# A decoder layer on one core: token-tile chains into the FFN in a written order on three engines, a third early unit, scale rows on the sync queue, and an opening ordered by hand

## The chip, the cores and the metric

The kernel runs on one core of a Trainium2 chip. The core has five engines that run side by side and wait for each other by semaphores: TensorE (PE, matrix products into PSUM), VectorE (DVE), ScalarE (ACT), GpSimd (POOL) and SyncE (SP). DMAs are issued from SP's and from ACT's queue; an engine that issues a DMA does so in its own order, between its other instructions. The metric is the device time of one execution in microseconds (us); less is better.

## What is computed

One layer of a decoder trunk on 512 tokens of width 1024: a mixer (mLSTM heads beside a gated convolution), then a gated FFN with a causal convolution of three taps. Both are sandwich-normed (an RMS norm before and one after), and scale, shift and gate of each come from a conditioning vector c through the matrix ada_w (adaLN). The parts around the change:

```python
mod = silu(c) @ ada_w[l] + ada_b[l]
sh1, sc1, g1, sh2, sc2, g2 = jnp.split(mod[:, None, :], N_MOD, axis=-1)
u = rms_norm(x, mix_pre_g[l]) * (1.0 + sc1) + sh1
proj = u @ w_in[l]
...
mix = jnp.concatenate([h, y], axis=-1) @ w_out[l]
x = x + g1 * rms_norm(mix, mix_post_g[l])

u = rms_norm(x, ffn_pre_g[l]) * (1.0 + sc2) + sh2
up = causal_dwconv(u @ ffn_up[l], ffn_conv_w[l], ffn_conv_b[l])
a, gt = jnp.split(up, 2, axis=-1)
f = (jax.nn.silu(gt) * a) @ ffn_down[l]
x = x + g2 * rms_norm(f, ffn_post_g[l])
```

D_FF is 2816, so the FFN has 22 units of 128 channels in each of its halves a and gt. All arrays are float32.

## The kernel before

**Precision and tiles.** Every large product is made from operands split into a high and a low part (float32r): `mm3` (L164) issues hi·hi, hi·lo and lo·hi into one PSUM bank. A weight block of 1 MB is loaded by SP into one of two `raw` buffers and split by `w_split` (L142) in four pieces: ACT copies the high part, POOL subtracts it for the low part. Split pieces lie in `wpool` (20 tiles) or in `slots` (44 tiles of 128 x 512, which also hold most activations). PSUM has eight banks: four `mm`, two `at`, and two that belong first to `cps` and later to the `cv` pool.

**Order.** SP and TensorE issue in the order in which the program is written. The order on DVE, ACT and POOL is made by a planner from its own simulated timeline, in which instructions that are written earlier have priority unless a written dependency or a raised priority number says otherwise.

**Opening (L105 to L290).** SP loads c, broadcast to 128 partitions (L105), some vectors (L107), the eight half tiles of x (L209), and then by turns a 1 MB pair of adaLN rows (`first_load`, L199, into the two `raw` buffers) and a block of glu weights (L269). ACT squares the half tiles with a sum (L226); DVE and POOL make a factor for each token (L228, L229); DVE scales the tile (L231); TensorE transposes it (`turn_x`, L218) into eight banks xT0 to xT7, of which xT6 and xT7 need banks that xT0 to xT3 leave. ACT and DVE copy them out by turns (L240, L242). For each of eight blocks k, DVE multiplies the adaLN rows by silu(c) and sums (`junk`, L279), makes scale and shift `gsk` (L282, L283), ACT makes the high part of u and the exact u (L285, L286), POOL its low part (L287), and TensorE runs 18 matmuls into six banks. The later adaLN products (`ada_block`, L125) are loaded by ACT's queue; the planner may put such an issue between ACT's other work.

**Into the FFN (L705 to L788).** The mixer's output is made in two column halves, mixa and mixb, with a bank for each of four token tiles. For mixb the first eight of sixteen weight blocks run over all tiles, then the rest tile by tile (8 x 3 matmuls each). Behind each tile comes its chain, `mix_tile` (L739): sums of squares on ACT (`sq_sum`, L552), a product with the g1 row on DVE, a factor (`token_factor`, L556: DVE, then POOL's power), the new x in two halves (L747), their squares on ACT, a second factor, then u in two steps for each half, a product with factor and the scale row `gs2r` (L752) and the addition of the shift row `sh2r` (L753, the second half on POOL). `turn_tile` (L756) transposes u into two `at` banks, and ACT and DVE make its high and low part. TensorE's order is: last part of mixb for tiles 0, 1, 2, transposes of tile 0, last part of tile 3, transposes of tile 1, then the early units.

The scale rows come by DMA: `send_rows` (L526) transposes the gains and writes them to DRAM, `row` (L535) reads them back broadcast over the partitions, both on ACT's queue. The two early units (0 and 1) run on half the tokens first, all four banks interleaved, with tile 2's transposes in the midst, then on the other half after tile 3's. From unit 2 on, a unit is 48 matmuls of 512 columns. Each unit's two banks are read by `conv3` (L796) on ACT and DVE, and a bank is free for a later unit when that is done. The adaLN products for g2 (blocks 40 to 47) are written at units 4, 8, 12 and 16 and have to follow `last_lo[0]`, an instruction of the last attention head.

## Time and profile before

| | |
|---|---|
| median of 3 runs | 831.38 us (827.21 to 833.15) |
| profiled execution, own time | 833.13 us |
| profiled execution, span from first to last instruction | 831.4 us |
| mean granted TensorE clock | 0.983 |
| HBM read, written | 102.60 MB, 4.21 MB |

The span is what the profile's clock counts; the execution's own time has some 1.7 us around it. A row of a timeline is: start in us, duration in us, engine, line of the kernel, operation, output<-inputs by tile name, shapes, count, and in brackets how long the engine was idle before it and which engine ended the wait. "ACTq" and "SPq" are the issuing of DMAs. A row of the table of windows is: the stretch, its length, then for PE, PE's weight loads, DVE, ACT and POOL the busy time with the number of instructions, then the granted TensorE clock (1.00 is full speed), the share of the DMA engines' time and GB/s.

### The profile page before, as it was taken

What the parts mean: (1) busy time and instruction counts of PE and PEld (TensorE: products, weight loads), DVE (VectorE), ACT (ScalarE), POOL (GpSimd) and SP (SyncE); (2) the same over time, 40 slices, a digit from 0 to 9 for tenths busy, and PEclk for the clock granted to TensorE, in tenths of its full rate; (3) what the DMA queues carried; (4) which work ended last, traced back from release to release, by engine and by line L of the source; (5) the groups of instructions that cost most, each with busy time, mean ns of one, the idle gap of its engine ahead of it and who ended that gap; (6) DMA issues with size and microseconds to landing.
All of it is one profiled execution on the core that took longest, in us unless ns stands there. A gap on an engine that the chain in (4) does not pass through costs nothing.

```text
span 831.4 us, 10237 instructions
## 1 busy us (share of the span) xinstructions
PE 788.3 (95%) x3713; PEld 654.9 (79%) x3713; DVE 473.7 (57%) x735; ACT 380.2 (46%) x710; POOL 448.2 (54%) x362
## 2 busy tenths in 40 slices
PE   3899999999999999999977979999999999999996
PEld 2688897778888888888866858888888888888885
DVE  4748999999997435548447664444444444000004
ACT  5665438757464454740434244444444444222211
POOL 2789749778596442541758334444444444444420
PEclk9999999999999999999988989999999999999999
DMA  7973214121237131518754522222222232222305
GB/s 275 330 274 126 101 52 152 51 90 64 76 103 256 61 113 52 203 51 300 289 196 142 162 102 84 83 91 98 101 102 102 102 126 102 99 83 80 119 1 177
DMA packets 25026, 107.47 MB, mean 129 GB/s; under 512 B 2928, under 2 KB 2960, under 8 KB 17552
## 3 DMA queue, kind: packets, MB, share of 16 engines
q1 hardware_dynamic: 16848, 83.73, 28.2%
q10 hardware_dynamic: 8128, 23.09, 7.8%
q8 instruction: 29, 0.48, 0.2%
q14 instruction: 21, 0.17, 0.1%
HBM read 102.60 MB, written 4.21 MB: 128 GB/s over the span
## 4 chain that ended last, share of the span: by engine, by line
PE 65%; DVE 16%; DMA 8%; issue 6%; POOL 3%; ACT 2%; SPq 0%; DVEq 0%; POOLq 0%; ACTq 0%
PE up L166 9%; PE up L167 9%; PE up L168 9%; DVE cv L605 8%; DMA ada<-in_adaT 5%; PE dn L168 5%; PE dn L166 5%; PE dn L167 5%; PE qko L166 4%; PE qko L168 4%; PE qko L167 4%; PE s L403 2%; PE o L414 2%; PE mixa L168 1%; PE mixa L166 1%
## 5 line engine op out<-in xcount | busy, mean ns | idle before, releaser
L605 DVE SCALAR_TENSOR_TENSOR cv<-gt,cvw,cv 128x488 f32<-128x488 f32 (+20 forms) x200 | 134.2, 725 | 2.8 <-issue 2.3
L872 DVE TENSOR_TENSOR fo<-dn,g2r 128x512 f32<-128x512 f32 x8 | 5.5, 691 | 100.1 <-PE dn L168 100.1
L149 POOL TENSOR_TENSOR wup_1024l<-wup,wup_1024h 128x512 fp32r<-128x512 f32 x22 | 29.4, 1334 | 42.0 <-ACT wup_1024h L148 42.0
L149 POOL TENSOR_TENSOR wup_1536l<-wup,wup_1536h 128x512 fp32r<-128x512 f32 x22 | 30.1, 1367 | 35.0 <-ACT wup_1536h L148 35.0
L601 POOL TENSOR_TENSOR cs<-cs,cs 128x510 f32<-128x510 f32 (+3 forms) x32 | 42.8, 1337 | 6.4 <-PE qko L168 4.5
L166 PE MATMUL up<-u2h,wup_0h 128*128 128x512 f32 (+1 forms) x96 | 37.0, 386 | 6.8 <-DVE fa0c L801 6.3
L149 POOL TENSOR_TENSOR wup_512l<-wup,wup_512h 128x512 fp32r<-128x512 f32 x22 | 28.4, 1289 | 24.5 <-ACT wup_512h L148 24.4
L149 POOL TENSOR_TENSOR wup_0l<-wup,wup_0h 128x512 fp32r<-128x512 f32 x22 | 29.0, 1318 | 19.2 <-ACT wup_0h L148 19.2
L167 PE MATMUL up<-u2l,wup_0h 128*128 128x512 f32 (+1 forms) x96 | 36.8, 383 | 0.7 <-DVE u2l L766 0.7
L168 PE MATMUL up<-u2h,wup_0l 128*128 128x512 f32 (+1 forms) x96 | 36.6, 381 | 0.0
L166 PE MATMUL up<-u2h,wup_512h 128*128 128x512 f32 (+1 forms) x96 | 36.4, 379 | 0.0
L133 DVE SCALAR_TENSOR_TENSOR junk<-ada,cb 128x1024 bf16<-128x1024 f32 x20 | 30.2, 1509 | 10.2 <-DMA ada<-in_adaT 9.9
L167 PE MATMUL up<-u2l,wup_512h 128*128 128x512 f32 (+1 forms) x96 | 36.0, 375 | 0.0
L167 PE MATMUL up<-u2l,wup_1536h 128*128 128x512 f32 (+1 forms) x96 | 35.9, 374 | 0.0
L168 PE MATMUL up<-u2h,wup_512l 128*128 128x512 f32 (+1 forms) x96 | 35.9, 374 | 0.0
L166 PE MATMUL up<-u2h,wup_1536h 128*128 128x512 f32 (+1 forms) x96 | 35.9, 374 | 0.0
L168 PE MATMUL up<-u2h,wup_1536l 128*128 128x512 f32 (+1 forms) x96 | 35.9, 374 | 0.0
L167 PE MATMUL up<-u2l,wup_1024h 128*128 128x512 f32 (+1 forms) x96 | 35.6, 371 | 0.0
L168 PE MATMUL up<-u2h,wup_1024l 128*128 128x512 f32 (+1 forms) x96 | 35.6, 371 | 0.0
L166 PE MATMUL up<-u2h,wup_1024h 128*128 128x512 f32 (+1 forms) x96 | 35.6, 371 | 0.0
L599 ACT ACTIVATE cs<-gt,cvw 128x511 f32<-128x511 f32 (+4 forms) x40 | 27.0, 715 | 9.4 <-POOL cs L601 8.2
L148 ACT ACTIVATE wup_512h<-wup 128x512 fp32r<-128x512 f32 x22 | 13.9, 632 | 37.5 <-PE up L167 35.6
(699 smaller groups left out, 2619.8 us busy)
## 6 DMA issues: line engine op xcount, KB each, us to landing
wup<-in_w_up SPq DMA_DIRECT2D x22, 1024.0 KB, 4.8
wqko<-in_w_qko SPq DMA_DIRECT2D x12, 1024.0 KB, 4.8
wd<-in_w_down SPq DMA_DIRECT2D x11, 1024.0 KB, 4.8
ada<-in_adaT ACTq DMA_DIRECT2D x20, 512.0 KB, 4.6
ada<-in_adaT SPq DMA_DIRECT2D x16, 512.0 KB, 6.5
wo<-in_w_out SPq DMA_DIRECT2D x8, 1024.0 KB, 4.8
spare<-in_adaT ACTq DMA_DIRECT2D x12, 512.0 KB, 7.4
wglu<-in_w_glu SPq DMA_DIRECT2D x5, 1024.0 KB, 6.1
```

The source lines that it names most:

```text
L133: t = V.scalar_tensor_tensor(out=junk, in0=r, scalar=1.0, in1=cb, op0=ALU.mult, op1=ALU.mult, accum_out=mod[:, i : i + 1])
L148: S.activation(hi[:, :n], src, AF.Copy)
L149: G.tensor_tensor(out=lo[:, :n], in0=src, in1=hi[:, :n].bitcast(F32), op=ALU.subtract)
L166: PE.matmul(ps, a[0], b[0], start=start, stop=False)
L167: PE.matmul(ps, a[0], b[1], start=False, stop=False)
L168: PE.matmul(ps, a[1], b[0], start=False, stop=stop)
L403: PE.matmul(sp[:, :n], ks[d][:, cc * P : (cc + 1) * P], qs[d][:, cc * P :], start=d == 0, stop=d == 1)
L414: PE.matmul(o[:, : DH + 2], E[h][cc][:, a : a + P], vs[h][cc], start=cc == 0, stop=cc == tt)
L599: S.activation(t[:, d:], cvx[j][:, : T - d], AF.Copy, scale=w(CK - 1 - d))
L601: G.tensor_tensor(out=side[:, d:], in0=side[:, d:], in1=t[:, d:], op=ALU.add)
L605: last_tap = V.scalar_tensor_tensor(out=cp[:, d:], in0=cvx[j][:, : T - d], scalar=w(CK - 1 - d), in1=cp[:, d:], op0=ALU.mult, op1=ALU.add)
L872: V.tensor_tensor(out=m, in0=banks[tt][hf], in1=g2r[hf], op=ALU.mult)
```

## The change

- **Opening.** c is loaded as two rows of one partition and broadcast by a product with ones on TensorE; both Silu read PSUM. x goes ahead of the vectors, half of it by ACT's queue. The second half of each tile is squared on DVE. All copies out of PSUM are on ACT, in a written order; for k=0 the high part of u is made straight from PSUM and its low part on DVE; for k=0 and 1 the products run in three passes over the six banks.
- **`in_order`.** A block that makes DVE, ACT and POOL issue its instructions in the order in which they are written. Instructions from outside the block may still be placed between them. It is put around the opening and around the chains into the FFN.
- **Chains.** `mix_tile` is cut into `chain_sums`, `chain_x` and `chain_u`; the product with `gs2r` moves ahead of the second factor, and factor and shift are one instruction on DVE. The four chains, the transposes, the splits of units 1 and 2 (low part on DVE) and the early units are written in one order. Three units run on half the tokens, a unit at a time; the third takes the two `cv` banks.
- **Rows.** gs2 and sh2 are written and read by SP's queue, between the loads of units 1 and 2. The g1 rows lie in the pool of v, u in the adaLN pool, and unit 1's weights in `slots`.
- **g2 blocks.** `last_lo[0]` is now the last low part of u2, so the products of blocks 40 to 47 have to follow it.

```diff
+    def in_order():
...
+        for ins in traced[a:]:
+            if ins.engine in (V.engine, S.engine, G.engine):
+                if ins.engine in last:
+                    tc.add_manual_dep(ins, last[ins.engine].name, mybir.DependencyInfo(mybir.DependencyClass.NoSync, mybir.DependencyReason.DATA),
+                                      reason="program order")
+                last[ins.engine] = ins
...
-    nc.sync.dma_start(cb, c.partition_broadcast(P))
...
+    for hf in range(2):
+        nc.sync.dma_start(crow[hf][:1, :], c[hf * T : (hf + 1) * T].rearrange("(a n) -> a n", a=1))
...
+    for tt in range(NT):
+        for hf in range(2):
+            (nc.scalar if hf else nc.sync).dma_start(xn[tt][hf], x[tt * P : (tt + 1) * P, hf * T : (hf + 1) * T])
...
-    S.activation(cps, cb, AF.Silu)
-    S.activation(cb, cb, AF.Silu)
+    for hf in range(2):
+        PE.matmul(cps[:, hf * T : (hf + 1) * T], ones[:1, :], crow[hf][:1, :], start=True, stop=True)
...
+    S.activation(first_silu, zero, AF.Silu)
...
-        G.tensor_tensor(out=lo[:, :n], in0=src, in1=hi[:, :n].bitcast(F32), op=ALU.subtract)
+        (eng or G).tensor_tensor(out=lo[:, :n], in0=src, in1=hi[:, :n].bitcast(F32), op=ALU.subtract)
...
+    first_load(0)
+    nc.sync.dma_start(vec[:, :FIRST], vecs[:, :FIRST])
...
+    def x_scale(tt, xs):
+        for hf in range(2):
+            V.tensor_scalar(out=xn[tt][hf], in0=xn[tt][hf], scalar1=xs[:, 1:], scalar2=None, op0=ALU.mult)
+            for i in range(NT if hf == 0 else 2):
+                turn_x(NT * hf + i, tt)
...
+    opening = in_order()
+    opening.__enter__()
...
     for tt in range(NT):
+        xsq = small.tile([P, 2], F32, tag="adap", name=f"xsq{tt}")
         for hf in range(2):
...
+            xjunk = xjunks[hf]
+            if hf:
+                V.scalar_tensor_tensor(out=xjunk, in0=xn[tt][hf], scalar=1.0, in1=xn[tt][hf], op0=ALU.mult, op1=ALU.mult, accum_out=xsq[:, hf:])
+            else:
+                S.activation(xjunk, xn[tt][hf], AF.Square, accum_out=xsq[:, :1])
+        if tt:
+            x_scale(tt - 1, xss[tt - 1])
+        if tt == 1:
+            S.activation(cb, cps, AF.Silu)
+        if tt == NT - 1:
+            S.activation(cps, cps, AF.Silu)
...
+        V.tensor_scalar(out=xs[:, :1], in0=xsq[:, :1], scalar1=xsq[:, 1:], scalar2=D * EPS, op0=ALU.add, op1=ALU.add)
+        G.tensor_tensor(out=xs[:, 1:], in0=xs[:, :1], in1=mhalf[:, :1], op=ALU.pow)
+        xss.append(xs)
+    x_scale(NT - 1, xss[-1])
...
-    for j in range(KT):
-        if j >= 6:
-            for tt in range(NT):
-                turn_x(j, tt)
-        if j % 2:
+    for j in range(6, KT):
+        for tt in range(NT):
+            turn_x(j, tt)
...
+        if k == 0:
+            for j in range(3):
+                x_out(j, S)
...
+        if k == 0:
+            x_out(3, S)
+            V.tensor_scalar(out=xr[0], in0=xr[0], scalar1=gsk[:, :1], scalar2=gsk[:, 1:], op0=ALU.mult, op1=ALU.add)
         hi, lo = u[k]
-        S.activation(hi, xr[k], AF.Identity, scale=gsk[:, :1], bias=gsk[:, 1:])
-        S.activation(xr[k], xr[k], AF.Identity, scale=gsk[:, :1], bias=gsk[:, 1:])
-        G.tensor_tensor(out=lo, in0=xr[k], in1=hi.bitcast(F32), op=ALU.subtract)
-        u[k] = (hi, lo)
-        for i, ps in enumerate(banks0):
-            mm3(ps, blk(wk, i), u[k], k == 0, k == KT - 1)
+        S.activation(hi, xT_ps[0] if k == 0 else xr[k], AF.Identity, scale=gsk[:, :1], bias=gsk[:, 1:])
+        if k:
+            S.activation(xr[k], xr[k], AF.Identity, scale=gsk[:, :1], bias=gsk[:, 1:])
+        (G if k else V).tensor_tensor(out=lo, in0=xr[k], in1=hi.bitcast(F32), op=ALU.subtract)
+        if k == 0:
+            for j in (6, 7, 4, 5):
+                x_out(j, S)
+        if k < 2:
+            for a, b in ((0, 0), (1, 0), (0, 1)):
+                for i, ps in enumerate(banks0):
+                    PE.matmul(ps, blk(wk, i)[a], u[k][b], start=k == 0 and a == b, stop=False)
+        else:
+            for i, ps in enumerate(banks0):
+                mm3(ps, blk(wk, i), u[k], False, k == KT - 1)
...
+    wide1 = vpool.tile([P, 2 * T + 8], F32, tag="vh", name="g1r")
+    g1r = row(0, lambda n: [wide1[:, :T], wide1[:, T : 2 * T]], "g1")
...
-    send_rows(KT, 2 * KT)
-    gs2r = row(1, cvtile, "gs2")
-    sh2r = row(2, cvtile, "sh2")
...
-    def mix_tile(tt):
+    def chain_sums(tt):
...
         ps = banks[tt]
         sq_sum(ps, msq[:, 2 * tt + 1 : 2 * tt + 2], f"mixb{tt}")
-        mb = slot(f"mgb{tt}")
-        V.tensor_tensor(out=mb, in0=ps, in1=g1r[1], op=ALU.mult)
-        r = token_factor(msq[:, 2 * tt : 2 * tt + 2], f"rm{tt}")
+        un = adas.tile([P, D], F32, tag="ada", name=f"un{tt}")
+        uns[tt] = [un[:, :T], un[:, T:]]
+        V.tensor_tensor(out=uns[tt][1], in0=ps, in1=g1r[1], op=ALU.mult)
+        return token_factor(msq[:, 2 * tt : 2 * tt + 2], f"rm{tt}")
...
+    def chain_x(tt, r):
...
-        for hf, m in enumerate((mg[tt], mb)):
+        for hf, m in enumerate((mg[tt], uns[tt][1])):
             V.scalar_tensor_tensor(out=x1[tt][hf], in0=m, scalar=r, in1=x1[tt][hf], op0=ALU.mult, op1=ALU.add)
             sq_sum(x1[tt][hf], xsq[:, hf : hf + 1], f"x1_{tt}_{hf}")
-        r2 = token_factor(xsq, f"rf{tt}")
-        for hf in range(2):
-            un = slot(f"un{tt}_{hf}")
-            V.scalar_tensor_tensor(out=un, in0=x1[tt][hf], scalar=r2, in1=gs2r[hf], op0=ALU.mult, op1=ALU.mult)
-            (G if hf else V).tensor_tensor(out=un, in0=un, in1=sh2r[hf], op=ALU.add)
-            uns[tt, hf] = un
+        for hf, un in enumerate(uns[tt]):
+            V.tensor_tensor(out=un, in0=x1[tt][hf], in1=gs2r[hf], op=ALU.mult)
+        return token_factor(xsq, f"rf{tt}")
...
+    def chain_u(tt, r):
+        for hf, un in enumerate(uns[tt]):
+            V.scalar_tensor_tensor(out=un, in0=un, scalar=r, in1=sh2r[hf], op0=ALU.mult, op1=ALU.add)
...
     def turn_tile(tt):
-        for hf in range(2):
-            un = uns[tt, hf]
...
+        turned[tt] = [atbank(f"xT{tt}_{hf}") for hf in range(2)]
...
             S.activation(hi, part, AF.Copy)
-            V.tensor_tensor(out=lo, in0=part, in1=hi.bitcast(F32), op=ALU.subtract)
...
-    up_w = {0: w_load(w_up[0], "wup0", slots, "t"), 1: w_load(w_up[1], "wup1")}
-    for tt in range(NT):
+            last_lo[0] = V.tensor_tensor(out=lo, in0=part, in1=hi.bitcast(F32), op=ALU.subtract)
+    def mix_last(tt, a, b):
         for n_, k in enumerate(MIX[KA:]):
-            mm3(banks[tt], (hy[k][0][:, tok(tt)], hy[k][1][:, tok(tt)]), wo[n_], False, n_ == 2 * KT - KA - 1)
-        mix_tile(tt)
-        if tt > 1:
-            turn_tile(tt - 2)
+            if a <= n_ < b:
+                mm3(banks[tt], (hy[k][0][:, tok(tt)], hy[k][1][:, tok(tt)]), wo[n_], False, n_ == 2 * KT - KA - 1)
...
+    def up_split(i, r, pool, tag):
+        q = len(up_w[i])
+        up_w[i].append(w_split(r[:, q * T : (q + 1) * T], f"wup{i}_{q * T}", pool, tag, V))
...
+    NE = 3
...
+    def up_half(th, i, only=None):
+        for half, ps in enumerate(early[i]):
+            if only not in (None, half):
+                continue
+            for k in range(KT):
+                mm3(ps[:, th * HT : (th + 1) * HT], blk(up_w[i], half * KT + k), (u2h[:, th, k, :], u2l[:, th, k, :]), k == 0, k == KT - 1)
...
+    up_w = {0: w_load(w_up[0], "wup0", slots, "t")}
+    raw1 = raw_up(1)
+    send_rows(KT, 2 * KT, nc.sync)
+    gs2r = row(1, cvtile, "gs2", nc.sync)
+    sh2r = row(2, cvtile, "sh2", nc.sync)
+    raw2 = raw_up(2)
+    early += [[mmbank(f"up{i}_{half}") for half in range(2)] for i in range(2)]
+    with in_order():
+        for tt in range(3):
+            mix_last(tt, 0, 2 * KT - KA)
+        up_split(1, raw1, slots, "t")
+        r = chain_sums(0)
+        up_split(1, raw1, slots, "t")
+        r = chain_x(0, r)
+        chain_u(0, r)
+        turn_tile(0)
+        mix_last(3, 0, 7)
+        r = chain_sums(1)
+        up_split(1, raw1, slots, "t")
+        r = chain_x(1, r)
+        chain_u(1, r)
+        turn_out(0)
+        turn_tile(1)
+        mix_last(3, 7, 2 * KT - KA)
+        r = chain_sums(2)
+        turn_out(1)
+        r = chain_x(2, r)
+        up_split(1, raw1, slots, "t")
+        chain_u(2, r)
+        up_half(0, 0)
+        turn_tile(2)
+        r = chain_sums(3)
+        up_split(2, raw2, wpool, "w")
+        r = chain_x(3, r)
+        up_split(2, raw2, wpool, "w")
+        chain_u(3, r)
+        up_half(0, 1)
+        up_split(2, raw2, wpool, "w")
+        early.append([cvbank(f"up2_{half}") for half in range(2)])
+        up_half(0, 2, 0)
+        turn_tile(3)
+        turn_out(2)
+        up_split(2, raw2, wpool, "w")
+        turn_out(3)
+    up_half(0, 2, 1)
+    for i in range(NE):
+        up_half(1, i)
...
-            turn_tile(3)
-        for k in range(KT):
-            if not th and k == KT // 2:
-                turn_tile(2)
-            for ps, i, half in early:
-                mm3(ps[:, th * HT : (th + 1) * HT], blk(up_w[i], half * KT + k), (u2h[:, th, k, :], u2l[:, th, k, :]), k == 0, k == KT - 1)
...
-        if i < 2:
-            pa, pg = early[2 * i][0], early[2 * i + 1][0]
+        if i < NE:
+            pa, pg = early[i]
```

`send_rows` and `row` take the queue as an argument, and use ACT's unless told otherwise.

More of the change, by code (lines that the diff above doesn't have):

```diff
@@ L1 @@
-from contextlib import ExitStack
+from contextlib import ExitStack, contextmanager
 import numpy as np
@@ L67, in decoder_layer @@
     psum = ctx.enter_context(tc.tile_pool(name="psum", bufs=1, space=PSUM))
+    @contextmanager
+    def in_order():
+        traced = nc.cur_bb.bb.instructions
+        first = traced[-1]
+        yield
+        a = next(i for i in reversed(range(len(traced))) if traced[i] is first) + 1
+        last = {}
+        for ins in traced[a:]:
[4 more added lines that the diff above has]
+                last[ins.engine] = ins
     def slot(name, dt=F32):
@@ L216, in decoder_layer, with x_out @@
     V.tensor_scalar(out=g32, in0=vcols("mix_pre_g", 0, KT), scalar1=RD, scalar2=None, op0=ALU.mult)
[L218 to L239 removed]
+    xr = [slot(f"xr{j}") for j in range(KT)]
+    for j in range(6, KT):
+        for tt in range(NT):
+            turn_x(j, tt)
+    def x_out(j, eng):
+        if eng is S:
             S.activation(xr[j], xT_ps[j], AF.Copy)
```

57 lines of the change are left out of this document (25 added, 32 removed).

## The prediction

> **What bounds the kernel now.** I read the page first, then the table of windows (busy time by stretch), then the timeline of each engine where that table shows TensorE idle.
>
> ```profile
> span 831.4 us, 10237 instructions
> PE 788.3 (95%) x3713; PEld 654.9 (79%) x3713; DVE 473.7 (57%) x735; ACT 380.2 (46%) x710; POOL 448.2 (54%) x362
> ```
> ```profile
> 0.00:25.00 25.00, 8.77 (x33) 6.35 (x33) 14.28 (x38) 15.06 (x30) 7.90 (x16) 1.00 0.82 288
> 25.00:140.00 115.00, 114.59 (x552) 96.79 (x553) 96.54 (x165) 64.88 (x114) 90.05 (x79) 1.00 0.46 165
> ...
> 428.00:433.00 5.00, 0.36 (x2) 0.19 (x2) 4.50 (x8) 1.38 (x4) 2.83 (x3) 0.86 0.15 57
> ...
> 449.00:456.00 7.00, 2.54 (x16) 2.37 (x15) 5.86 (x8) 0.71 (x3) 4.20 (x5) 0.72 0.41 146
> ...
> 460.00:464.00 4.00, 3.27 (x28) 3.10 (x27) 4.00 (x6) 0.00 (x0) 2.21 (x1) 1.00 0.62 183
> ...
> 468.00:477.60 9.60, 9.56 (x80) 9.36 (x78) 4.64 (x6) 2.34 (x4) 3.20 (x2) 1.00 0.51 170
> 477.60:484.00 6.40, 0.12 (x1) 0.15 (x1) 5.82 (x8) 2.75 (x5) 3.24 (x3) 0.90 0.50 164
> 484.00:490.00 6.00, 6.00 (x15) 4.71 (x16) 3.62 (x6) 1.68 (x3) 0.29 (x1) 0.53 0.01 3
> 490.00:800.00 310.00, 310.00 (x1368) 256.42 (x1368) 103.95 (x124) 120.19 (x196) 146.41 (x114) 1.00 0.26 95
> ```
>
> TensorE is the bound: 310 us without a gap from 490 to 800, 1368 matmuls, 0.227 us each at 512 columns (0.12 us each at 256, 80 in 9.56 us). Only time in which TensorE is idle or at half clock can be won, and the change touches just two such places: the first 25 us, and 428 to 490, where the token tiles pass from the mixer to the FFN. There 428:433, 449:456 and 477.6:484 are nearly empty, and after the pauses the clock column falls (0.53 in 484:490: 15 matmuls in 6 us where 26 would fit, 2.6 us lost).
>
> **The opening, step by step.** Rows of the windows and of the queues' timelines:
>
> ```profile
> 10.00:15.00 5.00, 3.67 (x15) 2.87 (x16) 3.25 (x10) 3.60 (x10) 1.92 (x4) 1.00 1.03 413
> ```
> ```profile
> 6.91 0.63 ACT L226 ACTIVATE xjunk<-xn 128x512 bf16<-128x512 f32 x1 [1.05 <-DMA xn<-in_x]
> ...
> 13.75 0.21 DVE L228 TENSOR_SCALAR xs<-xsq 128x1 f32<-128x1 f32 x1 [0.97 <-ACT xjunk L226]
> 13.88 0.87 DVE L231 TENSOR_SCALAR xn<-xn,xs 128x512 f32<-128x512 f32 x2
> ...
> 14.67 1.21 DVE L279 SCALAR_TENSOR_TENSOR junk<-ada,cps 128x1024 bf16<-128x1024 f32 x1
> ...
> 15.81 1.93 DVE L231 TENSOR_SCALAR xn<-xn,xs 128x512 f32<-128x512 f32 x2
> ...
> 18.92 0.80 SPq L203 DMA_DIRECT2D ada<-in_adaT  x2
> ...
> 25.23 0.80 PE L167 MATMUL glu<-ul,wglu_0h 128*128 128x512 f32 x1 [2.29 <-POOL ul L287]
> ...
> 28.40 0.20 DVE L283 TENSOR_SCALAR gsk<-adap,vec 128x1 f32<-128x1 f32 x1
> ...
> 47.02 3.13 ACTq L131 DMA_DIRECT2D ada<-in_adaT  x1
> ...
> 49.22 0.21 DVE L283 TENSOR_SCALAR gsk<-adap,vec 128x1 f32<-128x1 f32 x1
> ...
> 52.97 1.29 POOL L287 TENSOR_TENSOR ul<-xr,uh 128x512 fp32r<-128x512 f32 x1
> ...
> 59.25 0.39 PE L168 MATMUL glu<-uh,wglu_512l 128*128 128x512 f32 x1
> ```
>
> Before, the first half tile of x lands at 6.91 behind a 512 KB broadcast of c, eight squares run one after the other on ACT until 13.75, and DVE puts an adaLN product (14.67) between the last factor and its two scalings (15.81). Steady matmuls begin at 25.23, with the low part of u from POOL. The change loads c as two rows of 2 KB, which frees 1.3 us of transfer (512 KB at 413 GB/s), gives four of the eight squares to DVE, and keeps the products behind all scalings. The broadcast of c on TensorE and the second Silu from PSUM lie in idle time; vec, moved behind x and the first adaLN load on SP, is first read by bp1, after the last scaling. Four issues of x move to ACT's queue, which has nothing else to do then.
>
> The first tile, both halves, I put at 6.2, the others 1.3 apart (512 KB each). A tile costs DVE 0.7 for its square (half of 1.21, and a readout), 0.9 for two scalings (13.88), 0.2 for the factor: from tile 1 at 7.5 on DVE is the slower one, and tile 3's factor is out at 13.2. 0.96 later (the same three engines as 424.27 to 425.23 below) the scalings, to 14.9; two small operations and two products, 17.6; factors, 18.1; hi of u0 straight from PSUM, 0.8; first glu matmul at 19.2, its lo meanwhile on DVE. For k<2 all hi·hi products go first, so the 2.29 us wait for POOL disappears. With eight matmuls at 0.43 (cold) and ten at 0.227, k=0 ends at 24.9; before, k=1 began 7 x 18 x 0.227 = 28.6 ahead of the last matmul's end, 59.5, at 30.9. So 6 us at this point.
>
> But the later k are fed by two raw buffers of adaLN rows: the load for k=2 leaves when the products of k=0 end (18.92). From k=2 (28.40) to k=7 (49.22) the factors come every 4.16 us, and TensorE eats a k in 18 x 0.227 = 4.09. So what lasts is what the supply gains: 18.9 − 17.6 = 1.3 us, and the slack it had. k=7's lo of u ended at 54.26, late because ACT stood 3.13 us at a DMA issue of a later block (47.02). Without that it is 49.22 + 3.3 (hi, xr and POOL's lo: 0.8, 0.8, 1.29 and gaps) = 52.5, minus 1.3 = 51.2; the last matmul of k=7 starts sixteen later at 54.8, against 59.25: **4.4 us** gained. If ACT stops so again it is 2.7, and 0 if the written order itself stops once on a late load (low ends); if the supply never binds, 6.9 (high end: 6 and the wait's rest). I take 4.4, since the stop is of the planner's making and the loads keep their order. What follows up to 411 goes at TensorE's own pace or on chains that start from it, and shifts with it.
>
> **Into the FFN, step by step.**
>
> ```profile
> 420.17 1.29 POOL L149 TENSOR_TENSOR wup_1536l<-wup,wup_1536h 128x512 fp32r<-128x512 f32 x1
> ...
> 421.44 0.63 ACT L148 ACTIVATE wup_0h<-wup 128x512 fp32r<-128x512 f32 x1 [5.01 <-DMA wup<-in_w_up]
> ...
> 422.96 0.58 ACT L554 ACTIVATE mixb0junk<-mixb 128x512 bf16<-128x512 f32 x1
> ...
> 424.27 0.20 DVE L559 TENSOR_SCALAR rm0t<-msq 128x1 f32<-128x1 f32 x1
> ...
> 425.23 0.75 DVE L747 SCALAR_TENSOR_TENSOR x<-mg,rm0r,x 128x512 f32<-128x512 f32 x1 [0.77 <-POOL rm0r L561]
> ...
> 427.97 0.21 DVE L559 TENSOR_SCALAR rf0t<-xsq 128x1 f32<-128x1 f32 x1 [1.32 <-ACT x_1junk L554]
> ...
> 428.85 1.41 DVE L752 SCALAR_TENSOR_TENSOR un<-x,rf0r,gs2r 128x512 f32<-128x512 f32 x2
> ...
> 432.81 1.97 PE L761 MATMUL xT<-ident,un 128*128 128x128 f32 x8 [4.64 <-DVE un L753]
> ...
> 457.82 1.22 DVE L133 SCALAR_TENSOR_TENSOR junk<-ada,cb 128x1024 bf16<-128x1024 f32 x1
> ...
> 478.12 1.22 DVE L133 SCALAR_TENSOR_TENSOR junk<-ada,cb 128x1024 bf16<-128x1024 f32 x1 [1.58 <-DMA ada<-in_adaT]
> ...
> 481.68 0.74 DVE L801 SCALAR_TENSOR_TENSOR fa0c<-up,vec,fa0c 128x511 f32<-128x511 f32 x1
> ...
> 483.88 0.77 PE L166 MATMUL up<-u2h,wup_0h 128*128 128x512 f32 x1 [6.32 <-DVE fa0c L801]
> ...
> 497.54 0.39 PE L166 MATMUL up<-u2h,wup_0h 128*128 128x512 f32 x1
> ...
> 568.82 0.69 DVE L836 TENSOR_TENSOR fl<-fa8c,fh 128x512 fp32r<-128x512 f32 x1 [0.70 <-ACT fh L835]
> ```
>
> I keep the old clock times. ACT and DVE still begin with the split of unit 1, so with its load at 421.44: SP issues that load as before, and the scale rows wait behind it (issue about 419, 3 to 6 us to land, wanted at 425.7 and 427.8: covered by 1 to 2 us). Behind them SP has only unit 2's load, wanted at 444; ACT loses four issues. A split's lo costs 0.7 on DVE (568.82, the same operation) instead of 1.29 on POOL (420.17), so POOL has only the powers left.
>
> Tile 0: ACT split 0.54 and sums 0.67; DVE split 0.7 and product 0.65, factor at 423.35 (was 424.27); 0.96 to x as before; two x at 0.67, two products at 0.6, factor at 426.9; 0.88 more, and since gs2 now comes ahead of the factor only one step a half is left: transposes at 428.5. The second half waits for the bank of tile 1, freed by its product at 429.8. Done 430.35 (they began at 432.81 before). TensorE: 21 matmuls, 4.76, to 435.1. Tile 1 by the same prices: u at 435.6, banks free when both lo of tile 0 are out at 436.9; TensorE waits 1.2, then transposes and three matmuls to 438.2. From here it no longer waits: 48 x 0.12 = 5.8 a unit and half, transposes 1.1 each: 438.2 + 6 x 5.8 + 2 x 1.1 = **475.2** for unit 3. Tile 2 is ready at 443.8 (wanted 444.0), tile 3 at 450.3 (wanted 453.9). Before, unit 3 began at 497.54, so 22.3 us; the third unit's narrower matmuls (0.6 us more) are in it.
>
> The bank wait (483.88) came from the g2 blocks: eight products with DMA waits on DVE from 457.82, and behind them unit 0's taps at 481.68. Now they follow the last lo of u2 (about 456), and unit 0's taps, ready at 464, are wanted only at 475: 8 us of cover.
>
> The buffers that move (unit 1's halves to the slots, un to the adaLN pool, g1 to the v pool, unit 2's banks from the cv pool) cost no work. The slots just fit: 16 halves of the mixer's last eight blocks, 4 mg, 8 x1 and 16 of units 0 and 1 are 44; a wait would fall on unit 1's fourth split, made at 442 and wanted at 449.
>
> Two deductions. The clock:
>
> ```profile
> 150.00:160.00 10.00, 10.00 (x39) 7.41 (x39) 10.00 (x18) 5.89 (x10) 5.51 (x5) 0.83 0.29 106
> ```
>
> After some tiny matmuls the clock fell here, 39 matmuls instead of 46, 7 x 0.227 = 1.6 us; in 460:464, with 0.7 us idle, it didn't. My two pauses of some 1.2 us lie between: none to two falls, I take one, 1.6. ACT's stores of x1 between the squares: 1.0. 22.3 − 1.6 − 1.0 = **19.7**; bounds 8 (rivals below) and 22.3.
>
> [...]
>
> **Sum:** 4.4 + 19.7 = 24.1. The profiled execution took 833.13 us (span 831.4), 1.75 above the median of the runs; 833.13 − 24.1 = 809.0, against the median 831.38 it is 807.3. I predict 807.3.
>
> **Rivals.** (1) The g2 blocks again ahead of unit 0's taps: DVE is free at 456, and the planner may fill it. Eight blocks took 457.82 to 479.4, so taps about 480.3, bank 2.2 later at 482.5: 7.3 us of wait and 2.6 of clock, 9.9 less, 817. For it: it happened before; against: the taps are ready after two or three blocks. (2) The order doesn't matter, only data: transposes start no earlier than 432.81, and just the bank wait goes: 6.3 + 2.6 − 0.6 = 8.3, with the opening's 4.4 12.7, 819. For it: the same load at 421.44 heads both; against: two of the steps that go, a scaling on DVE and POOL's shift, lie between 427.97 and 432.81. (3) Both of these, or one with no gain in the opening: within 1%, 823 to 831. (4) Slower: the clock stays at half through the short-matmul stretch 428 to 475. That is 24 x 0.227 + 288 x 0.12 = 40 us of work, 40 us more: 847. It decides from 24 us on, 60% of that work. For it: 449:456 and 484:490 at 0.72 and 0.53; against: 460:464, pauses and 256-column matmuls at 1.00.
>
> [...]
>
> **Chances.** Forecast 0.68 (its own range 801 to 813: the high ends together, 29, and 19 gained), rival 1 0.12, rival 2 0.08, rival 3 0.06, rival 4 0.06. The range 799 to 819 holds the first three. A measurement here tells about 1% from no change; faster 0.88, same 0.06, slower 0.06.
>
> **What would show it.** Right: first glu matmul near 19, k=7 ending near 55; tile 0's transposes 47 us before unit 3 (65 before); no bank wait ahead of unit 3; windows of the transition near full at clock 1.00. Wrong: a new wait of ACT or DVE at the head of the written order, ada products ahead of the taps, or a clock near 0.5 over the early units.

## The result, and the profile after

| | before | after |
|---|---|---|
| median of the runs | 830.81 us (827.21 to 833.15, 4 runs) | 805.84 us (805.35 to 807.15, 4 runs) |
| profiled execution, own time | 833.13 us | 805.35 us |
| its span | 831.4 us | 803.4 us |
| mean granted TensorE clock | 0.983 | 0.993 |

The ratio of the times is 0.9706 (95% interval 0.9668 to 0.9743): faster by 2.9%, or 25.0 us in the medians. The forecast was 807.3 us. The first lines of the page after, and its table of windows (columns as before):

```profile
span 803.4 us, 10322 instructions
...
PE 786.0 (98%) x3765; PEld 654.2 (81%) x3765; DVE 477.3 (59%) x753; ACT 378.3 (47%) x706; POOL 438.0 (55%) x349
```
```profile
0.00:25.00 25.00, 19.66 (x62) 13.53 (x63) 17.70 (x51) 15.57 (x30) 10.62 (x18) 1.00 0.84 295
25.00:140.00 115.00, 111.54 (x532) 93.66 (x531) 97.20 (x166) 66.47 (x115) 92.37 (x80) 0.97 0.45 160
...
428.00:433.00 5.00, 5.00 (x27) 4.04 (x26) 3.43 (x7) 1.31 (x4) 0.54 (x1) 1.00 0.02 6
433.00:449.00 16.00, 15.83 (x133) 15.76 (x133) 14.04 (x25) 9.12 (x21) 4.71 (x5) 1.00 0.45 165
449.00:456.00 7.00, 7.00 (x61) 7.00 (x60) 4.09 (x5) 2.95 (x5) 4.73 (x5) 1.00 0.79 270
...
470.00:780.00 310.00, 310.00 (x1369) 256.67 (x1368) 106.16 (x132) 117.42 (x191) 146.63 (x112) 1.00 0.27 98
```

From 0 to 25 us TensorE is now busy for 19.66 us instead of 8.77, and of the three nearly empty stretches around 430, 450 and 480 nothing is left: full windows, and a clock of 1.00. The FFN itself (the last row, 1369 matmuls in 310 us) runs at the old pace. But 25:140 has become worse: 111.54 busy of 115 instead of 114.59, with a clock of 0.97. So the change gains in both of its places, and something in between takes a part back: the 0.97 is half clock for 6.8 us (134 to 141), and TensorE is idle for 3.5 us of the 115 where it was idle for 0.4.

Rows of the engines' timelines after, in the opening:

```profile
12.56 0.88 DVE L237 TENSOR_SCALAR xn<-xn,xs 128x512 f32<-128x512 f32 x2 [0.66 <-POOL xs L261]
...
14.77 1.22 DVE L319 SCALAR_TENSOR_TENSOR junk<-ada,cps 128x1024 bf16<-128x1024 f32 x1
...
16.02 0.80 SPq L225 DMA_DIRECT2D ada<-in_adaT  x2
...
17.22 2.08 PE L338 MATMUL glu<-uh,wglu_0h 128*128 128x512 f32 x4 [0.49 <-ACT uh L328]
...
33.22 0.50 PE L189 MATMUL glu<-ul,wglu_0h 128*128 128x512 f32 x1 [1.22 <-POOL ul L331]
...
54.23 0.39 PE L190 MATMUL glu<-uh,wglu_512l 128*128 128x512 f32 x1
```

The first steady matmul starts at 17.22. The load for k=2 leaves at 16.02, when the products of k=0 are done (18.92 before). Then TensorE meets a late factor again (1.22 us at 33.22, ended by the low part of u), and the last matmul of k=7 starts at 54.23 instead of 59.25: 5.0 us gained. In the transition:

```profile
412.46 0.63 ACT L170 ACTIVATE wup_0h<-wup 128x512 fp32r<-128x512 f32 x1 [2.67 <-DMA wup<-in_w_up]
414.94 0.60 ACT L606 ACTIVATE mixb0junk<-mixb 128x512 bf16<-128x512 f32 x1 [1.84 <-PE mixb L190]
...
425.56 1.03 PE L818 MATMUL xT<-ident,un 128*128 128x128 f32 x8
...
431.23 1.03 PE L818 MATMUL xT<-ident,un 128*128 128x128 f32 x8
...
433.24 0.39 PE L189 MATMUL up<-u2l,wup_0h 128*128 128x256 f32 x1 [0.17 <-DVE u2l L826]
...
448.47 1.04 PE L818 MATMUL xT<-ident,un 128*128 128x128 f32 x8
...
450.94 1.88 DVE L155 SCALAR_TENSOR_TENSOR junk<-ada,cb 128x1024 bf16<-128x1024 f32 x1
...
456.32 1.52 DVE L913 SCALAR_TENSOR_TENSOR fa0c<-up,vec,fa0c 128x511 f32<-128x511 f32 x2
...
469.49 0.40 PE L188 MATMUL up<-u2h,wup_0h 128*128 128x512 f32 x1
```

All four groups of transposes (425.56, 431.23 and 448.47 are shown) start without a wait, tile 0's 44 us ahead of unit 3, and the only wait left is 0.17 us at 433.24. The second g2 block and unit 0's taps follow each other at 455 to 457, and no bank is late at unit 3, which starts at 469.49.

Where the time went is read best from three marks: the last matmul ahead of `fcum` (the forget gate's sums, on the way into the attention), the transpose of the gains at the end of the mixer, and the first matmul of unit 3.

```profile
136.61 0.39 PE L497 MATMUL fcum<-g_lf,tri 128*128 128x4 f32 x2 [0.17 <-DVE g_lf L465]
...
411.36 0.27 PE L529 MATMUL gT<-ident,gains 128*16 128x128 f32 x1
```
```profile
133.13 0.39 PE L549 MATMUL fcum<-g_lf,tri 128*128 128x4 f32 x2 [1.71 <-DVE cs L650]
...
216.86 1.47 PE L491 MATMUL hT<-ident,hn 128*128 128x128 f32 x8 [1.46 <-DVE hn L485]
...
409.08 0.27 PE L581 MATMUL gT<-ident,gains 128*16 128x128 f32 x1
```

| mark | before | after | gained so far |
|---|---|---|---|
| k=7, last matmul | 59.25 | 54.23 | 5.0 |
| last matmul ahead of fcum | 136.05 | 131.03 | 5.0 |
| transpose of the gains | 411.36 | 409.08 | 2.3 |
| unit 3 | 497.54 | 469.49 | 28.05 |
| end of the span | 831.4 | 803.4 | 28.0 |

So the opening gained 5.0 us, of which 2.3 reached the mixer's end; the transition gained 25.8 (86.2 us from gains to unit 3 before, 60.4 after). These are single executions: the one before took 833.13 us, 2.3 above its median, the one after 805.35, 0.5 below, so the spans differ by 28.0 us where the medians differ by 25.0. The row at 133.13 names `cs`, a memset of 0.06 us; the operand itself, `g_lf`, is written by the DVE instruction ahead of it, which ended at 133.07.

### The profile page after: what moved, and what is told of

Read it like the earlier page. It is cut to its first block, busy times and chain, and to the rows that moved or that the text cites. A ratio compares the mean times of both kernels' runs of the same rounds, so it can differ in the third digit from the quotient of the medians.

```text
span 803.4 us, 10322 instructions
## 1 busy us (share of the span) xinstructions
PE 786.0 (98%) x3765; PEld 654.2 (81%) x3765; DVE 477.3 (59%) x753; ACT 378.3 (47%) x706; POOL 438.0 (55%) x349
## 4 chain that ended last, share of the span: by engine, by line
PE 86%; DVE 7%; DMA 2%; issue 1%; ACT 1%; POOL 1%; DVEq 0%; SPq 0%; POOLq 0%; ACTq 0%
PE up L189 10%; PE up L188 10%; PE up L190 10%; PE dn L190 5%; PE dn L188 5%; PE dn L189 5%; PE qko L188 4%; PE qko L190 4%; PE qko L189 4%; DVE cv L657 3%; PE glu L189 3%; PE glu L190 3%; PE glu L188 3%; PE s L455 2%; PE mixa L190 2%; PE mixa L188 2%
## 5 line engine op out<-in xcount | busy, mean ns | idle before, releaser
L657 DVE SCALAR_TENSOR_TENSOR cv<-gt,cvw,cv 128x506 f32<-128x506 f32 (+23 forms) x200 | 134.0, 728 | 1.8 <-ACT cv L645 1.5
L653 POOL TENSOR_TENSOR cs<-cs,cs 128x510 f32<-128x510 f32 (+3 forms) x32 | 43.8, 1369 | 3.5 <-ACT cs L651 3.4
L171 POOL TENSOR_TENSOR wup_1024l<-wup,wup_1024h 128x512 fp32r<-128x512 f32 x20 | 27.9, 1396 | 30.9 <-ACT wup_1024h L170 30.9
L171 POOL TENSOR_TENSOR wup_1536l<-wup,wup_1536h 128x512 fp32r<-128x512 f32 x20 | 26.3, 1317 | 29.0 <-ACT wup_1536h L170 29.0
L171 POOL TENSOR_TENSOR wup_512l<-wup,wup_512h 128x512 fp32r<-128x512 f32 x20 | 27.8, 1390 | 23.4 <-ACT wup_512h L170 23.4
L171 POOL TENSOR_TENSOR wup_0l<-wup,wup_0h 128x512 fp32r<-128x512 f32 x20 | 27.0, 1349 | 20.7 <-ACT wup_0h L170 20.7
L155 DVE SCALAR_TENSOR_TENSOR junk<-ada,cb 128x1024 bf16<-128x1024 f32 x20 | 31.9, 1593 | 6.1 <-DMA ada<-in_adaT 5.9
L171 POOL TENSOR_TENSOR wd_1024l<-wd,wd_1024h 128x512 fp32r<-128x512 f32 x11 | 14.2, 1292 | 29.6 <-ACT wd_1024h L170 29.6
L171 POOL TENSOR_TENSOR wqko_1024l<-wqko,wqko_1024h 128x512 fp32r<-128x512 f32 x12 | 15.6, 1304 | 26.1 <-PE v L189 14.5
```

Of the source, the lines that this page charges most:

```text
L155: t = V.scalar_tensor_tensor(out=junk, in0=r, scalar=1.0, in1=cb, op0=ALU.mult, op1=ALU.mult, accum_out=mod[:, i : i + 1])
L171: (eng or G).tensor_tensor(out=lo[:, :n], in0=src, in1=hi[:, :n].bitcast(F32), op=ALU.subtract)
L653: G.tensor_tensor(out=side[:, d:], in0=side[:, d:], in1=t[:, d:], op=ALU.add)
L657: last_tap = V.scalar_tensor_tensor(out=cp[:, d:], in0=cvx[j][:, : T - d], scalar=w(CK - 1 - d), in1=cp[:, d:], op0=ALU.mult, op1=ALU.add)
```

## Experiments

Each kernel was timed against the kernel before. The finest measure of the transition is the time from the transpose of the gains to unit 3 in the profile, called the passage below (before 86.2, after 60.4).

**The two parts alone.** `e1_open_only` has everything up to the end of the opening from the changed kernel and the rest from the one before; `e2_tail_only` the reverse.

> The opening of the changed kernel in front of the old way into the FFN. Theory 1, the parts add up: the last matmul of k=7 starts at 54.2 as in the changed kernel (59.25 before), some of the 5.0 us is given back before the mixer, and the time is 2.3 to 5.0 us below before, 826 to 828.5. Theory 2, the gain of the opening is eaten up by waits on DVE further on: 830 to 832. Theory 3, the early opening also moves the transition (the load of unit 1 came 9 us earlier against TensorE in the changed kernel): 820 to 825.

> The old opening, and the changed way into the FFN. Theory 1, the parts add up: unit 3 starts 60.4 us behind the transpose of the gains (86.2 before), 25.8 us gained, 804.5 to 806; with the opening's last 2.3 us this makes the whole. Theory 2, the load of unit 1 comes early only because of the new opening: it lands about 10 us behind the gains as before, the written order starts with that wait as I had forecast, unit 3 is 64 to 67 us behind the gains, 808.5 to 812.

| | median, us | ratio to before (95%) | gains transposed | passage |
|---|---|---|---|---|
| e1_open_only | 827.86 | 0.9966 (0.994 to 0.9992) | 408.19 | 86.1 |
| e2_tail_only | 805.69 | 0.969 (0.9643 to 0.9736) | 410.26 | 60.4 |
| both (the change) | 805.84 | 0.9706 (0.9668 to 0.9743) | 409.08 | 60.4 |

The first theory fits both: the opening alone wins 2.9 us (0.7 to 5.0 by the interval), the way into the FFN alone 25.0 (21.9 to 29.7). Together that would be 27.9, and the change wins 25.0; the intervals are too wide to say whether the time loses a part. The profiles show what happens to the opening's gain on the way: from the last matmul ahead of `fcum` to the gains, called the middle below, it takes 275.3 us before and 275.1 in `e2_tail_only` (from 135.18), but 278.1 after and 276.4 in `e1_open_only` (from 131.84). Two things are mixed in these numbers. In every profile the clock stands at 0.50 for one to three stretches of about 3.4 us between 133 and 159 (by windows of 2 us), and in each of them TensorE loses half of it, 1.7 us (its matmuls of 512 columns start 0.43 us apart there, in the kernel after from 137.22 to 140.63, and 0.23 at 1.00). With that taken off, the profiles, those of the runs below included, fall into groups:

| profiles | middle | of it at half clock | less half of that |
|---|---|---|---|
| old opening: before, `e2_tail_only` | 275.3, 275.1 | 3.4 | 273.6, 273.4 |
| new opening: after, e1, e3 to e8, e11 | 276.4 to 279.6 | 3.4, 6.8 or 10.2 | 274.5 to 274.7 |
| `e12_open_free` | 278.9 | 10.2 | 273.8 |
| `e9_gate_first` | 277.2 | 6.8 | 273.8 |
| `e10_both` | 275.8 | 6.8 | 272.4 |

So the new opening makes the middle about 1 us longer, and steadily so. The rest is the clock, and it differs between executions: `e8_g2_early` takes 276.4 and `e5_load_late` 279.6, with the same source up to the gains. Of the 2.7 us that are missing at the gains after the change, about 1.0 is of the first kind and 1.7 is a second stretch of half clock. Whether the new opening brings more such stretches, two profiles of the old one can't tell. The early load of unit 1 belongs to the tail: it is there in `e2_tail_only` (its first split at 413.60, 3.3 us behind the gains), and not in `e1_open_only` (418.71, 10.5 behind).

**The written order around the chains.**

```diff
-    with in_order():
+    if True:
         for tt in range(3):
```

> The changed kernel without the written order around the chains: the planner orders DVE, ACT and POOL there; all else as changed. Theory 1, the written order carries the gain: splits go ahead of steps of a chain again, TensorE waits for transposes, and the time is 811 to 821. Theory 2, the order is only a safeguard, and the gain comes from the work itself (one step less a half, splits off POOL, rows off ACT, units one at a time): 804.5 to 807.5.

814.98 us (ratio 0.9803, 0.9765 to 0.9841), passage 70.5: 10.1 us worse. The order carries more than a third of the passage's gain. What the planner does instead, on ACT and on DVE, and TensorE's longest wait:

```profile
418.26 0.63 ACT L606 ACTIVATE x_0junk<-x 128x512 bf16<-128x512 f32 x1 [2.59 <-DVE x L802]
...
422.52 0.63 ACT L170 ACTIVATE wup_0h<-wup 128x512 fp32r<-128x512 f32 x1 [3.54 <-DMA wup<-in_w_up]
...
423.06 0.62 ACT L606 ACTIVATE x_1junk<-x 128x512 bf16<-128x512 f32 x1
...
436.27 1.74 DVE L171 TENSOR_TENSOR wup_1024l<-wup,wup_1024h 128x512 fp32r<-128x512 f32 x1
...
437.94 1.75 DVE L171 TENSOR_TENSOR wup_1536l<-wup,wup_1536h 128x512 fp32r<-128x512 f32 x1
...
440.81 0.68 DVE L826 TENSOR_TENSOR u2l<-xT,u2h 128x512 fp32r<-128x512 f32 x1
...
441.55 0.58 PE L189 MATMUL up<-u2l,wup_0h 128*128 128x256 f32 x1 [3.76 <-DVE u2l L826]
```

Between the two squares of tile 0 (418.26 and 423.06) it puts the split of the next unit, whose load has not landed, and ACT stands for 3.54 us. Tile 0's transposes then wait only 0.69 us (at 426.45). The long wait, 3.76 us at 441.55, is for tile 1's low part, and ahead of that DVE does two more splits of unit 2 (436.27 and 437.94, 1.75 us each) and a product. A wait of 2.35 us for ACT (437.40) and half clock for 6.8 us (from 438.8 on) come on top. Splits ahead of the steps of a chain, with their load waits, are what the changed kernel's order shuts out.

**The supply of the opening.** A third buffer, in the pool of v, for the rows of k=2 and 5:

```diff
-        r = raws.tile([P, 2048], F32, tag="raw", name=f"ada{k}")
+        if k % 3 == 2:
+            r = [vpool.tile([P, 2 * T + 8], F32, tag="vh", name=f"ada{k}_{i}")[:, :D] for i in range(2)]
+        else:
+            raw = raws.tile([P, 2048], F32, tag="raw", name=f"ada{k}")
+            r = [raw[:, i * D : (i + 1) * D] for i in range(2)]
```

> The changed kernel with a third buffer (in the pool of v, idle then) for the adaLN rows of k=2 and 5. Theory 1, two raw buffers limit the supply of the later k: the last matmul of k=7 starts at 51.8 to 53 instead of 54.2; 1 to 2.4 us less at that point, and as much of it in the time as DVE lets through before the mixer, 803.5 to 806. Theory 2, the rate of the transfers or the products limit it: 54.2 as before, 805 to 807.

802.75 us (ratio 0.9659, 0.9623 to 0.9694), so 3.1 us less than the changed kernel and 0.75 below the range of the first theory; the profile's span is 1.7 us shorter (801.7).

```profile
52.24 0.39 PE L190 MATMUL glu<-uh,wglu_512l 128*128 128x512 f32 x1
...
131.13 0.39 PE L553 MATMUL fcum<-g_lf,tri 128*128 128x4 f32 x2 [1.71 <-DVE cs L654]
...
407.06 0.27 PE L585 MATMUL gT<-ident,gains 128*16 128x128 f32 x1
```

The last matmul of k=7 starts at 52.24 instead of 54.23. Two buffers were the limit. And these 2.0 us come through whole to the gains (407.06 instead of 409.08): the wait ahead of `fcum` stays 1.71 us, so DVE, which starts on the results of the opening, moved with it. Less the half clock (6.8 us in both) the middle is 274.6 us here as after the change. What it takes back beside the clock is therefore a fixed price and not "all that TensorE gains".

**Four parts of the passage, each undone alone.**

```diff
 e5_load_late
-    raw1 = raw_up(1)
     send_rows(KT, 2 * KT, nc.sync)
     gs2r = row(1, cvtile, "gs2", nc.sync)
     sh2r = row(2, cvtile, "sh2", nc.sync)
+    raw1 = raw_up(1)
     raw2 = raw_up(2)
 e6_split_pool
-        up_w[i].append(w_split(r[:, q * T : (q + 1) * T], f"wup{i}_{q * T}", pool, tag, V))
+        up_w[i].append(w_split(r[:, q * T : (q + 1) * T], f"wup{i}_{q * T}", pool, tag))
 e7_rows_act
-    send_rows(KT, 2 * KT, nc.sync)
-    gs2r = row(1, cvtile, "gs2", nc.sync)
-    sh2r = row(2, cvtile, "sh2", nc.sync)
+    send_rows(KT, 2 * KT)
+    gs2r = row(1, cvtile, "gs2")
+    sh2r = row(2, cvtile, "sh2")
 e8_g2_early
-            last_lo[0] = V.tensor_tensor(out=lo, in0=part, in1=hi.bitcast(F32), op=ALU.subtract)
+            V.tensor_tensor(out=lo, in0=part, in1=hi.bitcast(F32), op=ALU.subtract)
```

> The changed kernel with the load of unit 1 issued behind the scale rows on SP. In the changed kernel it is issued at 407.54 and its first split runs at 412.46, ahead of the sums of tile 0 at 414.94; here the issue comes at about 414.5 and the split at about 419.4. Theory 1, this load is the head of the written order, and my forecast was too high because it had come 9 us earlier than I assumed: tile 0's chain starts 4 to 5 us later, its 3 us of slack and the 0 of tile 1 leave 2 to 5 us of waits on TensorE, and a half clock may follow: 808 to 812. Theory 2, the chains have more slack than that, the load is no matter: 805 to 807.

> The changed kernel with the low parts of units 1 and 2 on POOL instead of DVE. Theory 1, POOL's 1.3 us of a split stands ahead of a power in the written order and lengthens each chain by 0.6 us for each, while TensorE has no slack at tile 1: 1 to 4 us of waits, 806.5 to 810. Theory 2, DVE is the fuller engine (6.9 of 8 us in 422 to 430), and taking 0.7 us a split off it makes good what POOL takes: 804.5 to 806.5.

> The changed kernel with the scale rows gs2 and sh2 written and read by ACT's queue, at the same place of the program. Theory 1, ACT stands at the issues (it waits there for the gains and for the write to DRAM, some 2 us each) ahead of the sums of tile 0, and the chains start late: 807 to 811. Theory 2, ACT is idle for 4 us ahead of the sums, and the issues fit there: 805 to 806.5.

> The changed kernel with the g2 blocks bound to the last head of the attention as before, so the planner may put their products anywhere behind it. Theory 1, they come ahead of the taps of unit 0, or between the steps of the chains, with their transfers' waits on DVE, which can wait for nothing else then: 811 to 818, and a bank wait ahead of unit 3 or transposes that come late. Theory 2, the cover of the third early unit (some 15 us between the taps and unit 3) takes them: 805 to 807.

| | median, us | ratio to before (95%) | passage | over the changed kernel's |
|---|---|---|---|---|
| e5_load_late | 810.37 | 0.9767 (0.9739 to 0.9795) | 65.3 | 4.9 |
| e8_g2_early | 808.42 | 0.9747 (0.9718 to 0.9776) | 64.2 | 3.8 |
| e6_split_pool | 806.17 | 0.9714 (0.969 to 0.9738) | 62.0 | 1.6 |
| e7_rows_act | 806.09 | 0.9715 (0.9689 to 0.9741) | 60.8 | 0.4 |

Load late: the first theory. The split at the head of the order stands for the load, later than I had expected (423.57, not 419.4), and TensorE waits at tile 0, 2.95 us in two pieces; half clock for 3.4 us goes with it (0.83 in 430 to 440):

```profile
423.57 0.63 ACT L170 ACTIVATE wup_0h<-wup 128x512 fp32r<-128x512 f32 x1 [11.83 <-DMA wup<-in_w_up]
```
```profile
430.96 0.66 PE L818 MATMUL xT<-ident,un 128*128 128x128 f32 x4 [2.34 <-DVE un L810]
...
432.22 1.11 PE L818 MATMUL xT<-ident,un 128*128 128x128 f32 x4 [0.61 <-DVE un L795]
```

g2 blocks early: the first theory's mechanism, but small; the time lies between the two ranges. DVE does a block (442.11, 0.61 us for its transfer) ahead of tile 3's last step, and TensorE waits 1.93 us for a bank at tile 3's transposes; a clock of 0.83 in 450 to 460 follows (1.7 us of 10). The two make 3.6 of the 3.8. Unit 0's taps and unit 3 are not held up.

```profile
442.11 1.23 DVE L155 SCALAR_TENSOR_TENSOR junk<-ada,cb 128x1024 bf16<-128x1024 f32 x1 [0.61 <-DMA ada<-in_adaT]
```
```profile
448.71 1.25 PE L818 MATMUL xT<-ident,un 128*128 128x128 f32 x8 [1.93 <-DVE u2l L826]
```

Splits on POOL and rows on ACT: their medians are within 0.3 us of the changed kernel's, too little for these runs to tell, and in the range of the second theory each; in the passage the splits cost 1.6, at the low end of the first theory's waits, the rows 0.4. So the queue of the rows doesn't matter here: ACT had the time, as the second theory said.

The four and the order were each undone alone, and their prices (10.7 and 10.1 us of the passage) need not add up. What the rest of the edit is worth, the step less in each half of a chain and the units one at a time above all, was not separated.

**Two early units.** `NE = 2`, the splits and the first halves of unit 2 taken out of the order, unit 2 run as the later ones.

> The changed kernel with two units on half the tokens instead of three; unit 2 runs as the later ones. Theory 1, the third unit is cover: without it TensorE waits for the low part of tile 3 (1 to 2 us) and unit 2 for the banks of unit 0, whose taps are then wanted 5 to 6 us earlier: 808 to 812, with a half clock. Theory 2, order and g2 blocks alone keep the banks free, the third unit only costs its narrower matmuls (0.6 us): 804.5 to 806.5.

817.56 us (ratio 0.9843, 0.9814 to 0.9873), worse than either theory, and for another reason:

```profile
418.57 0.63 ACT L606 ACTIVATE x_0junk<-x 128x512 bf16<-128x512 f32 x1 [2.21 <-DVE x L802]
...
422.24 0.63 ACT L170 ACTIVATE wup_0h<-wup 128x512 fp32r<-128x512 f32 x1 [2.95 <-DMA wup<-in_w_up]
...
422.78 0.61 ACT L606 ACTIVATE x_1junk<-x 128x512 bf16<-128x512 f32 x1
```
```profile
455.30 1.97 PE L818 MATMUL xT<-ident,un 128*128 128x128 f32 x8 [6.21 <-DVE u2l L826]
```

Unit 2's splits, no longer written inside the order, are instructions from outside, which the planner may place in it: ACT waits 2.95 us for unit 2's load between the squares of tile 0, and on POOL three splits stand ahead of a power of tile 3. TensorE waits 6.21 us at tile 3's transposes, and half clock for 6.8 us goes with it (0.66 in 450 to 460). The run shows that the order protects only what is written in it. What the third unit is worth as cover for the banks it does not show: no bank wait is seen ahead of unit 2.

**The opening's order.** The two lines that open and close the written order there are taken out.

> The changed kernel without the written order in the opening, which the planner orders again; loads, passes and all operations as changed. Theory 1, the order is what keeps the adaLN products behind the scalings and the hi of u0 early: first glu matmul 1 to 3 us later than 17.22, but k=7 ends no more than 1 us later, since the supply limits it: 805.5 to 808. Theory 2, a product or a DMA issue gets in the way of the later k as before (the last matmul of k=7 at 56 to 59): 807 to 810.

803.4 us (800.52 to 805.59; ratio 0.9673, 0.9639 to 0.9707). Both theories miss: the planner does no worse than the written order. First matmul at 16.97, k=7's last at 53.65. The gain of the opening is that of its loads and operations; which of them, was not taken apart.

**The middle.** Taps on DVE that the planner had put between the forget gate's small operations follow the last of them, `g_lf`; alone, and with the third buffer:

```diff
+            if j > 3 or (j == 3 and d > 25):
+                tc.add_manual_dep(last_tap.ins, g_lf.ins.name, mybir.DependencyInfo(mybir.DependencyClass.NoSync, mybir.DependencyReason.DATA),
+                                  reason="order on VectorE")
```

> The changed kernel, with the forget gate's small operations on DVE (L511 to L517) ahead of the conv taps that the planner had put between them: taps of block 3 from d=26 on and of all later blocks follow the last of them. Theory 1, the part of the opening's gain that is missing at the mixer's end goes to the 1.71 us wait of TensorE for this chain and to the half clock behind it, and both are the planner's order: no wait there, clock 1.00 behind it, gains transposed at 404 to 407 instead of 409.08, the time 801 to 804. Theory 2, DVE is full up to 225 and what it gives up here TensorE waits for later: 805 to 807.

> The third buffer of the run above and the gate's chain first, together. Theory 1, both are independent: 2 us from the buffer and 2 to 5 from the order, 797.5 to 801. Theory 2, DVE takes one of them back: 802 to 804.

804.22 us (ratio 0.9681, 0.9652 to 0.971) and 802.27 us (0.9662, 0.9638 to 0.9687).

```profile
129.15 1.22 DVE L517 SCALAR_TENSOR_TENSOR g_lf<-gz,g_fl 128x16 f32<-128x16 f32 x1
...
140.67 1.17 DVE L552 TENSOR_TENSOR ga<-gz,Fc 128x16 f32<-128x16 f32 x1
```
```profile
131.63 0.28 PE L549 MATMUL fcum<-g_lf,tri 128*128 128x4 f32 x2
...
141.89 1.13 PE L557 MATMUL aT<-ident,ga 128*4 128x128 f32 x8 [2.37 <-DVE ga L552]
```

`g_lf` ends 2.7 us earlier (130.37 instead of 133.07), and the wait ahead of `fcum` is gone; but the next link, `ga`, is late now, and TensorE, here still at full clock, waits 2.37 us ten us later. The gains are transposed at 408.57, 0.5 us earlier, and with the third buffer at 406.32 instead of 407.06. The clock hides a part of it: less half clock the middle is 0.9 us shorter than after the change, and 2.2 with the third buffer (272.4 against 274.6). So a part of a wait taken from DVE at one place comes back at the next; how large a part, two profiles can't tell. 804.22 lies between the two theories; its four runs (803.24 to 804.91) are all below those of the changed kernel. Both kernels with the third buffer beat the changed kernel; between them, 802.27 (the second theory's range) and 802.75, these runs can't tell.

## Why the prediction was right

The time, 805.84, lies 1.5 us from the forecast, and that is closer than the sum deserves. Two of its terms were wrong with opposite sign: at the gains the opening's 4.4 is 2.3, and the transition's 19.7 is 25.8. That makes 28.1 in these two profiles, where 24.1 was forecast. The medians differ by only 25.0, since these two executions lie 2.3 above and 0.5 below them. So the places of the gain were right, and the nearness of the number is in part luck. (The low end of the forecast's own range, 29 us under the median, is 802, not 801.)

- **First matmul and end of k=0.** Forecast 19.2, measured 17.22. The tiles of x came earlier (first square at 4.16, not 6.2), and DVE's last scaling ended at 13.44, not 14.9. k=0 ended at 23.4, forecast 24.9. The forecast's 0.43 and 0.227 us are the pace of the kernel before from 25.82 to 28.81 and from there on; after, the first six matmuls took 2.7 us (17.22 to 19.94), the last six 1.4 (21.99 to 23.38), with the clock column at 1.00 in both kernels.
- **Supply by two buffers.** Forecast: k=7's last matmul at 54.8, 4.4 us gained. Measured 54.23, 5.0. The limit was the right one: a third buffer moved it by 2.0. The way there was not: the load for k=2 left 2.9 us earlier than before, not 1.3, but the factors then came every 4.50 us (24.27 for k=2 to 46.77 for k=7), not every 4.16. ACT's stop at an issue was gone, as forecast (0.33 us at 49.20 instead of 3.13).
- **"What follows up to 411 goes at TensorE's own pace or on chains that start from it, and shifts with it."** This step failed. 2.7 of the 5.0 us were gone at the gains, about 1.0 in the middle itself and 1.7 as a second stretch of half clock (the table in the experiments). TensorE reached `fcum` 5.0 us earlier, DVE's chain for it came only 3.5 earlier; then followed half clock, and at 216.86 another DVE wait of 1.46 us. The windows quoted in the prediction held the warning: DVE busy 96.54 of 115 us in 25:140. In `e9_gate_first` one wait was taken away and the next link was late. DVE's chain, from `g_fu` to the end of `g_lf`, began 5.4 us earlier (123.37 against 128.73) and took 9.7 us instead of 7.8: its six small operations took 3.9 us against 3.1 (two of them 1.16 and 1.32 instead of 0.10 and 0.16, see the last section), and the planner put a `ydl` of 1.12 us ahead of `g_lf`, which stood behind it before. Together that is the 1.9. What of this reaches the gains is the 1.0; at half clock TensorE came to the next link, `aT`, without a wait, where it waited 1.39 us before.
- **Head of the written order.** I kept unit 1's load at 421.44, 10.1 us behind the gains. It was 3.4 behind (412.46), and the chain waited for its own matmuls instead (414.94). The planner now splits the last group of w_out ahead of the sums on ACT (399.55, before 410.73), so the raw buffer is free earlier; `e2_tail_only` shows that this comes with the tail, and `e3_tail_free` that it isn't the written order. Which of its edits does it is open. With the load late, `e5_load_late` has the passage at 65.3, 20.9 us better than before; the forecast for that state was 22.3 ahead of deductions, 20.7 with the one for a fall of the clock, which happened there, and 19.7 with both.
- **Waits and deductions.** 1.2 us of wait at tile 1, 1.6 for one fall of the clock and 1.0 for the stores: measured 0.17 us of wait, clock 1.00 from 410 on, and the stores between the squares cost 0.25 us, covered. The term of the sum that was mis-sized is the transition: 19.7 forecast, 25.8 measured. Of the 6.1 between them 2.6 are the two deductions, and 3.1 lie ahead of unit 0, whose first matmul came 23.7 us behind the gains (432.80), not 26.8 (438.2): the early load and no wait at tile 1.
- **Rival 1**, the g2 blocks: run as `e8_g2_early`, where it costs 2.6 us in the time and 3.8 in the passage, not 9.9. It struck tile 3, not unit 0's taps.
- **Rival 2**, the order doesn't matter: false, the order is worth 10.1 us of the passage; but 15.7 of the 25.8 came without it.
- **Rival 3**, both of these or an opening without gain, 823 to 831: not seen.
- **Rival 4**, half clock through the short matmuls: not seen (433:449 and 449:456 at 1.00). The changed kernel, where TensorE waited only 0.17 us, doesn't show what a longer pause between such matmuls does. In `e8_g2_early`, where TensorE waited 1.93 us, the clock was at half for 3.4 us from 450 on and then at 1.00 again among the 256-column matmuls (0.21 us each up to 453.4, then 0.12).

## What to carry to other kernels

A gain ahead of a stretch in which another engine is nearly full is not wholly a gain at the end (here, of 5.0 us at k=7, 2.3 were left at the gains: 1.7 went to half clock and about 1.0 to DVE's chain, with DVE busy for 97.20 of 115 us in 25:140): look at the busy share of the second engine before shifting everything behind by the same amount. A chain of short steps on three engines is worth an order written by hand when a wait for a load can be planned into it, and then the splits that wait for loads must be written into the order too, each behind its landing. Find what the head of a new order waits for, and ask what the edit itself does to that time. Before a few us between two profiles are given a cause, take off what each lost at half clock: here that was 1.7 to 5.1 us in the same stretch, between programs with the same source up to there.
